# A four-layer transformer on one core: relative-position biases stored once, down rows paired, scores negated, scalings merged, block bias from Toeplitz tiles

## The chip, the core and the metric

The kernel runs on one core of one Trainium2 chip. Times are device microseconds (us) of one execution. Engines are called by their short names: PE is TensorE (PEld its weight loads), DVE VectorE, ACT ScalarE, POOL GpSimd, SP SyncE. A source line L196 is line 196 of the kernel before.

## The reference, cut to what matters

256 tokens of width 1,024 pass through four layers in float32. Layer 0 mixes by two kinds of attention (8 heads causal in one block, 8 heads dilated), layer 1 by a sparse attention of three branches (compressed, selected, windowed), and each of them is followed by a dense feed-forward net of 2,816 and a gated product. Layers 2 and 3 mix by attention in a band of 128 tokens with one sink per head beside a short convolution, followed by 32 experts of 512 of which each token uses two.

```python
s = einsum('bhqd,bhkd->bhqk', q, k) * HEAD_DIM ** -0.5 + tab[:, _rel_bucket(t_q - t_k)]
pr = exp(s - max(s)) / sum(exp(s - max(s)))          # masked to t_q >= t_k
o = einsum('bhqk,bhkd->bhqd', pr, v)
# layer 1, compressed branch: 15 keys, key c of tokens 16c .. 16c+31
dc = t[:, None] - (16 * arange(15) + 31)             # masked to dc >= 0
s = einsum('bghsd,bgcd->bghsc', qg, kc) * HEAD_DIM ** -0.5 + tabg[:, :, _rel_bucket(dc)]
# layers 2 and 3: sink in max and sum; experts: (silu(x @ gate) * (x @ up)) @ down
```

The bias depends on the distance of query and key alone, so a head's bias is one row of 256 numbers, and its 128 x 256 tile is that row shifted by one for each query: a Toeplitz tile.

## The kernel before, in words

The program is written out by hand: each engine runs its instructions in the order in which the Python code emits them, and waits on semaphores where a tile is not ready.

**Weights.** `Ring` loads them in pieces of 1 MB on SP's queue into a few slots (5 in the first two layers, with 8, 3 and 2 more from other pools later) in one fixed order; a piece is issued when a slot comes free. In the dense parts `Split` halves a piece into a high and a low part: ACT rounds it (`whi`, L196), DVE or, while `split.second` says so, POOL subtracts (`wlo`, L204), and PE multiplies three times (`mm3`, L332 to L334). The experts use the ring's pieces directly (L1728, L1752). Gate and up pieces have 8 KB in a row for each partition, down pieces two rows of 4 KB that lie 512 KB apart.

**Order.** `Side` holds generators that go a step further at each `tick`; a `yield 4` waits for four ticks. Layer 0 (`mixer0`) projects q, k, q, k and v in turn, PE working through pieces of the ring. Beside this `bias_rows` multiplies the table with a one-hot matrix, so that each head has its row (16 rows for the first kind, 8 with the dilation's weights), and POOL's queue writes each row 128 times to HBM (`rows_d`, 24 x 128 x 384). `bias_tiles` then reads a tile of four heads with a step of 383, which shifts each partition's row by one (`T`, two buffers, POOL's queue); the first two loads wait for the writes.

**Attention.** Units of two heads run through `Attention.run` at staggered offsets: scores on PE, `att_bias` on DVE (score plus bias, with the maximum of each row; L684, L686; then the maximum negated, L689), `att_exp` on ACT (L695, L696), `att_scale` on DVE (reciprocal, for layer 1 times the gate, then four scalings, L701 to L706), `att_transpose` on PE, `att_take` on ACT and DVE (`ta`, `tb`), values on PE. The output projection fills PE between the steps, with POOL subtracting its low parts. There are 8 units in layer 0 and 16 in layer 1.

**Behind layer 0's attention** `block_bias` loads two one-hot tiles on POOL's queue. In `last_steps` PE turns token tile 0, then makes 32 products of 32 rows by 16 columns (L979) for the bias of the compressed keys, which DVE adds to a mask (`cbias`), then turns token tile 1 (L369; ACT and DVE take the result, L381, L376, L385, L389), and `rest(0)` begins its feed-forward net (FFN 0), whose first product needs both tiles.

**Layers 2 and 3.** `mixer` does the banded attention inside a `Side` generator while the convolution's products fill PE; its scores are scaled by four instructions (L1385). `moe` takes the experts in pairs; `turn` transposes the activations of an expert in two halves of 128 columns (L1739), which meet the two down rows of a partition.

## Time and profile before

| | us |
|---|---|
| median of 3 runs | 1999.36 (1996.43 to 2000.14) |
| the profiled execution | 2000.12, its span 1998.4 |
| PE busy | 1816.1 (91%) |
| DVE busy | 835.6 (42%) |
| ACT busy | 679.5 (34%) |
| POOL busy | 135.8 (7%) |
| mean granted clock of PE | 0.968 |
| DMA | 559.15 MB, mean 280 GB/s over the span |

Matmuls are pipelined and their ends are modelled, so a busy PE is not PE at its peak. [...] The shares are means over stages with different limits.

### The profile page before, as it was taken

What the parts mean: (1) busy time and instruction counts of PE and PEld (TensorE: products, weight loads), DVE (VectorE), ACT (ScalarE), POOL (GpSimd) and SP (SyncE); (2) the same over time, 40 slices, a digit from 0 to 9 for tenths busy, and PEclk for the clock granted to TensorE, in tenths of its full rate; (3) what the DMA queues carried; (4) which work ended last, traced back from release to release, by engine and by line L of the source; (5) the groups of instructions that cost most, each with busy time, mean ns of one, the idle gap of its engine ahead of it and who ended that gap; (6) DMA issues with size and microseconds to landing.
All of it is one profiled execution on the core that took longest, in us unless ns stands there. A gap on an engine that the chain in (4) does not pass through costs nothing. (4 is left out here: it accounts for less than half of the span.)

```text
span 1998.4 us, 29447 instructions
## 1 busy us (share of the span) xinstructions
PE 1816.1 (91%) x11967; PEld 1399.4 (70%) x11967; DVE 835.6 (42%) x1918; ACT 679.5 (34%) x1415; POOL 135.8 (7%) x126
## 2 busy tenths in 40 slices
PE   8489999999889999997899999997897999998996
PEld 6367999877669998886677676563685777675553
DVE  6264655565866555695121121111684111121112
ACT  6154644564666445653111111111552111111111
POOL 0033000033320000200000000000110000000000
PEclk9788999999999999998999999999998999999999
DMA  9842655544226554574999999999845999999996
GB/s 248 164 151 83 232 190 191 168 131 146 71 64 232 190 193 166 175 273 166 379 417 417 416 416 417 416 417 402 315 169 203 388 416 416 417 416 417 417 416 272
DMA packets 170173, 559.15 MB, mean 280 GB/s; under 512 B 10176, under 2 KB 69992, under 8 KB 137200
## 3 DMA queue, kind: packets, MB, share of 16 engines
q1 hardware_dynamic: 167056, 546.47, 71.1%
q0 software_dynamic: 2976, 10.74, 3.2%
q8 instruction: 96, 1.57, 0.3%
q14 instruction: 45, 0.37, 0.1%
HBM read 551.40 MB, written 5.77 MB: 279 GB/s over the span
## 5 line engine op out<-in xcount | busy, mean ns | idle before, releaser
L1728 PE MATMUL wps<-wring,X 128*64 128x256 f32 x4096 | 480.6, 381 | 15.5 <-DMA wring<-in_w_expert_up_dram 15.3
L1728 PEld LDWEIGHTS wps<-wring,X 128*64 128x64 f32 x4096 | 336.3, 137 | 148.3 <-DMA wring<-in_w_expert_up_dram 30.4
L204 DVE TENSOR_TENSOR wlo<-wring,whi 128x1024 fp32r<-128x1024 f32 (+1 forms) x247 | 257.5, 1085 | 99.2 <-ACT whi L196 98.8
L196 ACT CAST whi<-wring 128x1024 fp32r<-128x1024 f32 (+1 forms) x283 | 254.8, 945 | 58.6 <-DMA wring<-in_w_in_ab_dram 39.7
L1752 PE MATMUL wps<-wring,aT 128*64 128x512 f32 x1024 | 250.6, 596 | 16.9 <-DMA wring<-in_w_expert_down_dram 16.9
L332 PE MATMUL wps<-xh,whi 128*128 128x256 f32 x832 | 236.0, 284 | 2.6 <-ACT xh L376 2.6
L333 PE MATMUL wps<-xl,whi 128*128 128x256 f32 x832 | 233.8, 281 | 1.4 <-DVE xl L389 1.4
L334 PE MATMUL wps<-xh,wlo 128*128 128x256 f32 x832 | 233.5, 281 | 0.0
L1733 DVE TENSOR_TENSOR a<-a,wps 128x256 f32<-128x256 f32 x64 | 27.0, 421 | 464.7 <-ACT a L1732 464.7
L1752 PEld LDWEIGHTS wps<-wring,aT 128*64 128x64 f32 x1024 | 116.9, 136 | 119.6 <-issue 49.9
L1732 ACT ACTIVATE a<-wps 128x256 f32<-128x256 f32 x64 | 24.6, 385 | 437.4 <-PE wps L1728 437.4
L332 PEld LDWEIGHTS wps<-xh,whi 128*128 128x128 f32 x832 | 157.6, 189 | 8.6 <-issue 3.3
L333 PEld LDWEIGHTS wps<-xl,whi 128*128 128x128 f32 x832 | 157.2, 189 | 3.3 <-DVE xl L389 1.9
L332 PE MATMUL acc<-whi,xh 128*128 128x512 f32 (+1 forms) x360 | 149.7, 416 | 8.9 <-ACT whi L196 8.9
L334 PEld LDWEIGHTS wps<-xh,wlo 128*128 128x128 f32 x832 | 157.8, 190 | 0.0
L1761 DVE SCALAR_TENSOR_TENSOR yl<-wps,gs,yh 128x512 fp32r<-128x512 f32 x64 | 48.0, 751 | 254.3 <-ACT yh L1760 252.7
L334 PE MATMUL acc<-whi,xl 128*128 128x512 f32 (+1 forms) x360 | 144.9, 402 | 8.2 <-DVE xl L389 7.9
L333 PE MATMUL acc<-wlo,xh 128*128 128x512 f32 (+1 forms) x360 | 144.7, 402 | 2.8 <-DVE wlo L204 2.8
L1760 ACT ACTIVATE yh<-wps,gs 128x512 fp32r<-128x512 f32 x64 | 43.9, 688 | 230.2 <-PE wps L1752 220.1
L347 POOL TENSOR_SCALAR ss<-ss 128x1 f32<-128x1 f32 x22 | 5.4, 244 | 1453.5 <-ACT junk L345 1453.3
L204 POOL TENSOR_TENSOR wlo<-wring,whi 128x1024 fp32r<-128x1024 f32 (+1 forms) x36 | 88.1, 2461 | 134.5 <-ACT whi L196 78.8
L334 PEld LDWEIGHTS acc<-whi,xl 128*128 128x128 f32 x360 | 71.0, 197 | 27.4 <-DVE xl L389 9.7
(367 smaller groups left out, 2492.8 us busy)
## 6 DMA issues: line engine op xcount, KB each, us to landing
wring<-in_w_expert_gate_dram SPq DMA_DIRECT2D x128, 1024.0 KB, 18.8
wring<-in_w_expert_up_dram SPq DMA_DIRECT2D x128, 1024.0 KB, 19.8
wring<-in_w_expert_down_dram SPq DMA_DIRECT2D x128, 1024.0 KB, 20.0
wring<-in_w_ffn_gate_dram SPq DMA_DIRECT2D x22, 1024.0 KB, 9.5
wring<-in_w_ffn_up_dram SPq DMA_DIRECT2D x22, 1024.0 KB, 5.4
wring<-in_w_ffn_down_dram SPq DMA_DIRECT2D x22, 1024.0 KB, 7.1
wring<-in_w_in_dram SPq DMA_DIRECT2D x18, 1024.0 KB, 8.6
wring<-in_w_in_ab_dram SPq DMA_DIRECT2D x10, 1024.0 KB, 11.5
```

The source lines that it names most:

```text
L196: self.nc.scalar.copy(vh, src)
L204: eng.tensor_sub(vl, src, vh)
L332: nc.tensor.matmul(o, lh, rh, start=start, stop=False)
L333: nc.tensor.matmul(o, lh, rl, start=False, stop=False)
L334: nc.tensor.matmul(o, ll, rh, start=False, stop=stop)
L347: nc.gpsimd.tensor_scalar(ss, ss, 1.0 / D, EPS, ALU.mult, ALU.add)
L1728: nc.tensor.matmul(o[64 * half:64 * half + 64, lo:lo + 256], xg[:, k, 64 * (e % 4):64 * (e % 4) + 64], w[:, c, 256 * half:256 * half + 256 ...
L1732: nc.scalar.activation(a, o[:, 0:256], AF.Silu)
L1733: nc.vector.tensor_mul(a, a, o[:, 256:512])
L1752: nc.tensor.matmul(y[d2][64 * ab:64 * ab + 64, :], aTs[ab][:, j, 64 * hf:64 * hf + 64], ws[ab][:, j, 512 * d2:512 * d2 + 512], start=hf + ...
L1760: nc.scalar.activation(ys[0][:, s_], y[d2], AF.Copy, scale=g)
L1761: nc.vector.scalar_tensor_tensor(ys[1][:, s_], y[d2], g, ys[0][:, s_], ALU.mult, ALU.subtract)
```

## The change

- `rows_d` holds each head's row once: 24 rows of 383 numbers, 127 masked ones ahead of the 256 biases, which now run in the order of the distance. A tile is read with a step of 1 from partition to partition (`toeplitz`), and `att_bias` reads it backwards along the keys.
- All scores are negated (the factor on q is -0.125, biases and masks change sign). The least value takes the place of the greatest and is already the offset that the exponent needs, which ACT evaluates with scale -1. The negations (L689, L1366) go. In the mixers a negated copy of the sinks is made on POOL.
- `att_scale` multiplies both heads at once by a broadcast operand, two instructions in place of four; the mixers' scaling becomes one in place of four.
- `block_bias` goes into `rest(0)` as a `Side` generator: two memsets, then four times a `toeplitz` load on POOL's queue, four ticks, and two DVE copies that pick every 16th column. The 32 products, the one-hot tiles and the mask go.
- Down pieces give each partition two neighbouring rows, 8 KB in one run; `turn` transposes the even and the odd columns.

```diff
...
-    c2["wmask"] = np.where(np.abs(t[:, :, None] - k) <= 128, 0.0, NEG).astype(f).reshape(128, -1)
+    c2["wmask"] = np.where(np.abs(t[:, :, None] - k) <= 128, 0.0, -NEG).astype(f).reshape(128, -1)
...
-    c["cmask"] = np.where(ok, 0.0, NEG).astype(f).reshape(128, -1)
...
-    hot = (np.arange(32)[:, None] == b[::-1]).astype(f)
-    bc = np.where(ok, b[np.maximum(dc, 0)], 0)
-    hotc = (np.arange(32)[:, None, None, None] == bc.transpose(1, 2, 0)).astype(f)
-    d = np.arange(S)[::-1]
+    hot = (np.arange(32)[:, None] == b).astype(f)
+    d = np.arange(S)
...
-    return c, c2, np.concatenate([hot, hotc.reshape(32, -1)], 1), np.broadcast_to(lnc, (8, S)).copy()
+    return c, c2, hot, np.broadcast_to(lnc, (8, S)).copy()
...
-                    ring.add(("d", l, e, hf), [(0, (2, 1024), x["w_expert_down_2"][l, e, 256 * hf:256 * hf + 256, :].rearrange("(c p) n -> p c n", p=128))])
+                    ring.add(("d", l, e, hf), [(0, (2, 1024), x["w_expert_down_2"][l, e, 256 * hf:256 * hf + 256, :].rearrange("(p c) n -> p c n", c=2))])
...
+            def keys(j, n):
+                v = T[:, 2 * hp + j, n - 1:n]
+                return bass.AP(tensor=v.tensor, offset=v.offset, ap=[v.ap[0], [-1, n]])
...
-                nc.vector.tensor_tensor_reduce(out=p[:, j, 0:256], in0=sc[j][:, 0:256], in1=T[:, 2 * hp + j, :], scale=1.0,
-                                               scalar=-3.0e38, op0=ALU.add, op1=ALU.max, accum_out=m[:, j:j + 1])
-                nc.vector.tensor_tensor_reduce(out=p[:, j, 256:384], in0=sc[j][:, 256:384], in1=T[:, 2 * hp + j, 128:256], scale=1.0,
-                                               scalar=-3.0e38, op0=ALU.add, op1=ALU.max, accum_out=m[:, 2 + j:3 + j])
-            nm = small.tile([128, 4], F32, name="nm", tag="nm")
-            nc.vector.tensor_scalar(nm, m, -1.0, None, ALU.mult)
-            return p, nm
+                nc.vector.tensor_tensor_reduce(out=p[:, j, 0:256], in0=sc[j][:, 0:256], in1=keys(j, 256), scale=1.0,
+                                               scalar=3.0e38, op0=ALU.add, op1=ALU.min, accum_out=m[:, j:j + 1])
+                nc.vector.tensor_tensor_reduce(out=p[:, j, 256:384], in0=sc[j][:, 256:384], in1=keys(j, 128), scale=1.0,
+                                               scalar=3.0e38, op0=ALU.add, op1=ALU.min, accum_out=m[:, 2 + j:3 + j])
+            return p, m
...
-                nc.scalar.activation(p[:, j, 0:256], p[:, j, 0:256], AF.Exp, bias=nm[:, j:j + 1], accum_out=l[:, j:j + 1])
-                nc.scalar.activation(p[:, j, 256:384], p[:, j, 256:384], AF.Exp, bias=nm[:, 2 + j:3 + j], accum_out=l[:, 2 + j:3 + j])
+                nc.scalar.activation(p[:, j, 0:256], p[:, j, 0:256], AF.Exp, scale=-1.0, bias=nm[:, j:j + 1], accum_out=l[:, j:j + 1])
+                nc.scalar.activation(p[:, j, 256:384], p[:, j, 256:384], AF.Exp, scale=-1.0, bias=nm[:, 2 + j:3 + j], accum_out=l[:, 2 + j:3 + j])
...
-            nc.vector.reciprocal(r, l)
...
+                nc.vector.reciprocal(r, l)
...
-            for j in range(2):
-                nc.vector.tensor_scalar(p[:, j, 0:256], p[:, j, 0:256], r[:, j:j + 1], None, ALU.mult)
-                nc.vector.tensor_scalar(p[:, j, 256:384], p[:, j, 256:384], r[:, 2 + j:3 + j], None, ALU.mult)
+            else:
+                nc.vector.reciprocal(r, l)
+            for i, s_ in enumerate((slice(0, 256), slice(256, 384))):
+                nc.vector.tensor_mul(p[:, :, s_], p[:, :, s_], r[:, 2 * i:2 * i + 2].unsqueeze(2).to_broadcast([128, 2, s_.stop - s_.start]))
...
+        def toeplitz(row, name, bufs):
+            t = ptile([128, 4, 256], F32, name, bufs=bufs)
+            nc.gpsimd.dma_start(t, bass.AP(tensor=rows_d.tensor, offset=rows_d.offset + row * 383, ap=[[1, 128], [383, 4], [1, 256]]))
+            return t
...
-                        tiles[i] = ptile([128, 4, 256], F32, "T")
-                        src = bass.AP(tensor=rows_d.tensor, offset=rows_d.offset + rows[i] * 128 * 384 + 127, ap=[[383, 128], [128 * 384, 4], [1, 256]])
-                        nc.gpsimd.dma_start(tiles[i], src)
+                        tiles[i] = toeplitz(rows[i], "T", 2)
...
-        def last_steps(i, outp, nxt, pp, pv, mid=None):
+        def last_steps(i, outp, nxt, pp, pv):
...
-            if mid:
-                fns.append(mid)
-            for k in sorted(range(len(fns)), key=lambda k: (15 if k == 5 else T1[11 + 6 * i + k])):
+            for k in sorted(range(len(fns)), key=lambda k: T1[11 + 6 * i + k]):
...
-        rows_d = dram.tile([24, 128, 384], F32, name="rows_d")
+        rows_d = dram.tile([24, 383], F32, name="rows_d")
...
-            nc.sync.dma_start(hot, x["hot"][:, 0:256])
+            nc.sync.dma_start(hot, x["hot"])
...
-            nc.gpsimd.memset(r1[:, 256:], NEG)
-            nc.gpsimd.memset(r2[:, 256:], NEG)
+            nc.gpsimd.memset(r1[:, :127], -NEG)
+            nc.gpsimd.memset(r2[:, :127], -NEG)
...
-            nc.vector.tensor_copy(r1[:, :256], pr[:16, 0:256])
-            nc.vector.tensor_add(r2[:, :256], pr[:8, 256:512], lnc)
-            nc.gpsimd.dma_start(rows_d[0:16], r1.unsqueeze(1).to_broadcast([16, 128, 384]))
-            nc.gpsimd.dma_start(rows_d[16:24], r2.unsqueeze(1).to_broadcast([8, 128, 384]))
+            nc.vector.tensor_scalar(r1[:, 127:383], pr[:16, 0:256], -1.0, None, ALU.mult)
+            nc.vector.scalar_tensor_tensor(r2[:, 127:383], pr[:8, 256:512], -1.0, lnc, ALU.mult, ALU.subtract)
+            nc.gpsimd.dma_start(rows_d[0:16], r1[:, :383])
+            nc.gpsimd.dma_start(rows_d[16:24], r2[:, :383])
...
-            hotc = [ptile([128, 16, 128], F32, "hotc", tag=tag, bufs=1) for tag in ("qT", "kT")]
-            for i in range(2):
-                nc.gpsimd.dma_start(hotc[i][:32].rearrange("p a b -> p (a b)"), x["hot"][:, 256 + 2048 * i:2304 + 2048 * i])
-            yield 0
-            pc = wps()
-            for i in range(32):
-                nc.tensor.matmul(pc[:, 16 * i:16 * i + 16], hotc[i // 16][:32, i % 16, :], M["tab"][:32, :], start=True, stop=True)
-            for t in range(2):
-                nc.vector.tensor_add(cbias[:, t], pc[:, 256 * t:256 * t + 256].rearrange("p (c h) -> p h c", c=16),
-                                     C["cmask"][:, 16 * t:16 * t + 16].unsqueeze(1).to_broadcast([128, 16, 16]))
-            yield 0
+            nc.gpsimd.memset(cbias[:, 0, :, 7:], -NEG)
+            nc.gpsimd.memset(cbias[:, 1, :, 15:], -NEG)
+            for q in range(4):
+                T = toeplitz(4 * q, "Tb", 1)
+                yield 4
+                for t, n in ((0, 7), (1, 15)):
+                    v = T[:, :, 16 * n - 16:16 * n - 15]
+                    nc.vector.tensor_copy(cbias[:, t, 4 * q:4 * q + 4, 0:n], bass.AP(tensor=v.tensor, offset=v.offset, ap=[v.ap[0], v.ap[1], [-16, n]]))
...
-                nc.vector.tensor_scalar(gq[:, i:i + 1], M[a], M[b], 0.125, ALU.mult, ALU.mult)
+                nc.vector.tensor_scalar(gq[:, i:i + 1], M[a], M[b], -0.125, ALU.mult, ALU.mult)
...
-            bb = block_bias()
-            next(bb)
...
-            last_steps(0, outp, nm, pp, pv, lambda: next(bb))
+            last_steps(0, outp, nm, pp, pv)
...
+                if i == 0:
+                    side.spawn(block_bias())
...
-            nc.vector.tensor_scalar(gq, M["qn_nsa"], 0.125, None, ALU.mult)
+            nc.vector.tensor_scalar(gq, M["qn_nsa"], -0.125, None, ALU.mult)
...
-                nc.vector.tensor_reduce(out=mx, in_=pc, axis=AX.X, op=ALU.max)
+                nc.vector.tensor_reduce(out=mx, in_=pc, axis=AX.X, op=ALU.min)
...
-                nc.scalar.activation(pc, pc, AF.Exp)
+                nc.scalar.activation(pc, pc, AF.Exp, scale=-1.0)
...
+            nsink = ptile([128, 8], F32, "nsink", bufs=1)
+            nc.gpsimd.tensor_scalar(nsink, sink, -1.0, None, ALU.mult)
...
-                                                       scalar=sink[:, 2 * hp + j:2 * hp + j + 1], op0=ALU.add, op1=ALU.max, accum_out=m[:, j, t:t + 1])
-                nc.vector.tensor_scalar(m, m, -1.0, None, ALU.mult)
+                                                       scalar=nsink[:, 2 * hp + j:2 * hp + j + 1], op0=ALU.add, op1=ALU.min, accum_out=m[:, j, t:t + 1])
...
-                        nc.scalar.activation(p[:, j, t], p[:, j, t], AF.Exp, bias=m[:, j, t:t + 1], accum_out=l_[:, j, t:t + 1])
+                        nc.scalar.activation(p[:, j, t], p[:, j, t], AF.Exp, scale=-1.0, bias=m[:, j, t:t + 1], accum_out=l_[:, j, t:t + 1])
...
-                for j in range(2):
-                    for t in range(2):
-                        nc.vector.tensor_scalar(p[:, j, t], p[:, j, t], l_[:, j, t:t + 1], None, ALU.mult)
+                nc.vector.tensor_mul(p, p, l_.unsqueeze(3).to_broadcast([128, 2, 2, 256]))
...
-                nc.scalar.activation(qT[:, :, 128 * t:128 * t + 128], pt.rearrange("p (c n) -> p c n", c=4), AF.Copy, scale=0.125)
+                nc.scalar.activation(qT[:, :, 128 * t:128 * t + 128], pt.rearrange("p (c n) -> p c n", c=4), AF.Copy, scale=-0.125)
...
-                    nc.tensor.transpose(pt[:, 128 * j:128 * j + 128], a[:, 128 * j:128 * j + 128], ident)
+                    nc.tensor.transpose(pt[:, 128 * j:128 * j + 128], a.rearrange("p (m j) -> p j m", j=2)[:, j], ident)
...
```

## Rows read from the trace of the kernel before

**Rows 1.** the page's slices: what the DMA engines moved, GB/s in 40 slices of 50 us

```profile
GB/s 248 164 151 83 232 190 191 168 131 146 71 64 232 190 193 166 175 273 166 379 417 417 416 416 417 416 417 402 315 169 203 388 416 416 417 416 417 417 416 272
```

**Rows 2.** windows: length, busy us and instructions by engine, TensorE's granted clock, DMA share, GB/s

```profile
20.00:60.00 40.00, 40.00 (x185) 31.59 (x184) 26.34 (x49) 19.28 (x29) 2.32 (x2) 1.00 1.01 181
60.00:110.00 50.00, 19.81 (x73) 14.88 (x73) 13.30 (x19) 12.52 (x18) 1.56 (x2) 0.66 0.76 199
```

**Rows 3.** DMA issues by line: engine, count, KB of each, median us from issue to landing

```profile
T<-rows_d POOLq DMA_DIRECT2D x8, 512.0 KB, 5.2
rows_d<-r POOLq DMA_DIRECT2D x1, 3072.0 KB, 37.5
rows_d<-r POOLq DMA_DIRECT2D x1, 1536.0 KB, 68.6
```

**Rows 4.** waits from 60 to 101 us: who waited for whom, total us, times, longest

```profile
ACT whi L196 <- DMA wring<-in_w_in_ab_dram: 39.0, 3, 23.3
```

**Rows 5.** timeline behind the first attention: start, us, engine, line, operation [idle <-releaser]

```profile
187.99 10.59 PE L979 MATMUL wps<-sm,hotc 32*128 32x16 f32 x64
189.34 0.92 ACT L376 CAST xh<-xn 128x256 fp32r<-128x256 f32 x2
198.51 1.97 PE L369 MATMUL wps<-idg,xn 128*128 128x128 f32 x8
199.66 0.63 ACT L381 ACTIVATE xn<-wps,sm 128x128 f32<-128x128 f32 x2 [9.40 <-PE wps L369]
200.77 0.58 PE L332 MATMUL wps<-xh,whi 128*128 128x256 f32 x1 [0.30 <-ACT xh L376]
```

**Rows 6.** windows over the two attentions, as rows 2

```profile
110.00:178.00 68.00, 58.51 (x310) 41.41 (x311) 36.63 (x131) 34.61 (x96) 32.57 (x22) 0.92 0.37 118
490.00:600.00 110.00, 93.30 (x608) 69.30 (x604) 84.60 (x313) 64.64 (x201) 34.80 (x29) 0.97 0.21 66
```

**Rows 7.** windows at the start of FFN 0, as rows 2

```profile
202.00:204.00 2.00, 1.98 (x9) 1.98 (x10) 1.73 (x3) 2.00 (x3) 0.00 (x0) 0.50 0.00 0
206.00:208.00 2.00, 2.00 (x19) 2.00 (x18) 2.00 (x3) 2.00 (x4) 0.00 (x0) 1.00 0.66 96
```

**Rows 8.** VectorE's groups, second attention: xcount | busy us, mean ns | idle before

```profile
L705 DVE TENSOR_SCALAR p<-p,r 128x256 f32<-128x256 f32 x32 | 13.6, 426 | 0.6
L689 DVE TENSOR_SCALAR nm<-m 128x4 f32<-128x4 f32 x16 | 12.5, 781 | 0.6
L706 DVE TENSOR_SCALAR p<-p,r 128x128 f32<-128x128 f32 x32 | 9.0, 280 | 0.0
L703 DVE TENSOR_TENSOR r<-r,gates 128x4 f32<-128x4 f32 x16 | 5.5, 344 | 0.5
```

**Rows 9.** VectorE's groups, first attention (110 to 178 us)

```profile
L689 DVE TENSOR_SCALAR nm<-m 128x4 f32<-128x4 f32 x8 | 7.7, 966 | 0.3
```

**Rows 10.** the negation alone: ns min/median/max, first and last start

```profile
L689 DVE TENSOR_SCALAR nm<-m x24: 170/171/2359, 112.1 to 573.7; 128x4 f32<-128x4 f32 x24
```

**Rows 11.** GpSimd's groups, 480 to 605 us

```profile
L204 POOL TENSOR_TENSOR wlo<-wring,whi 128x1024 fp32r<-128x1024 f32 x14 | 33.7, 2411 | 21.3 <-ACT whi L196 21.3
```

**Rows 12.** VectorE's two-input products by shape, 480 to 605 us

```profile
L389 DVE TENSOR_TENSOR xl<-xn,xh 128x256 fp32r<-128x256 f32 x4 | 1.6, 419 | 0.2 <-ACT xh L376 0.2
L389 DVE TENSOR_TENSOR xl<-xn,xh 128x512 fp32r<-128x512 f32 x2 | 1.4, 693 | 0.1
```

**Rows 13.** waits of TensorE's weight loads, second attention

```profile
PEld wps L725 <- DVE tb L719: 6.6, 6, 2.6
```

**Rows 14.** the mixers' scalings: ns min/median/max, first and last start

```profile
L1385 DVE TENSOR_SCALAR X<-X,l x32: 340/348/753, 850.1 to 1476.4; 128x256 f32<-128x256 f32 x32
```

**Rows 15.** DMA queues, 1848.3 to 1858.5 (down) and 1860 to 1878 us: packets, MB, share

```profile
q1 hardware_dynamic: 973, 4.21, 102.6%
...
q1 hardware_dynamic: 1123, 7.50, 100.6%
```

**Rows 16.** expert weight issues from 1590 to 1960 us: ns, first and last start

```profile
L143 SPq DMA_DIRECT2D wring<-in_w_expert_down_dram x51: 367/379/2440, 1592.5 to 1957.9; - x51
```

## The prediction, made before the changed kernel was run

> **What bounds the kernel now.** I read the slices of the page first, for the stages. HBM traffic stands near 417 GB/s from 1,000 to 1,400 us and again from 1,600 to the end: the two expert stages run at the speed of the DMA engines [rows 1]. Before 1,000 us the traffic is lower and TensorE sets the pace, with one exception at the start: between 60 and 110 us the traffic sags and TensorE does little. The windows show it: 73 matmuls in those 50 us at a granted clock of 0.66, against 185 in the 40 us before at 1.00 [rows 2]. The issues say why: the two writes of `rows_d`, 3.0 and 1.5 MB out of 16 and 8 partitions, take 37.5 and 68.6 us to land [rows 3], and meanwhile the first projection's weights are late: ScalarE, which rounds them, waits 39.0 us for them in three waits [rows 4]. The reader should see that nothing else is due in that stretch. Third, the timeline behind the first attention: the 32 small products of `block_bias` stand between the turns of token tile 0 and of tile 1, and FFN 0 begins only after both [rows 5]. Fourth, the two attention stages: TensorE is busy 58.5 of 68 and 93.3 of 110 us, VectorE 84.6 of the 110 [rows 6].
>
> **The change part by part.** The sum is made against the profiled execution's 2000.1 us, 0.8 above the median of 1999.4.
>
> *Biases once.* The writes shrink from 4.5 MB to 24 rows of 1.5 KB, 37 KB in all; at any rate the trace shows that is hidden under the projections. Then 60 to 110 us goes at the pace of 20 to 60 us: 73 matmuls at 40/185 us each are 15.8 us instead of 50.0, a gain of 34.2. What hides the weights afterwards is the same ring that kept TensorE 100% busy from 20 to 60 us [rows 2]. Bounds: if the clock stays where it was, the busy 19.8 us remain and 30.2 are gained; if transposes, which are shorter, count less, 36.
>
> *Block bias moved.* [...] Without it the transposes of tile 1 go at 188.0 instead of 198.5. ScalarE is busy with tile 0 until 190.26 and then needs the 1.1 us from 199.66 to 200.77 again, so FFN 0 starts at 191.4 instead of 200.77: 9.4. FFN 0 then began at half clock (9 matmuls in 2 us at 202, 19 at 206 [rows 7]); some 3 us of it at twice the speed are 1.5 more. I take 10.8; 8.3 if the wait after the transposes stays 2.26 us behind ScalarE's last cast, 12 at best. The step moves into FFN 0: two memsets, four loads of 512 KB on GpSimd's queue and eight copies of at most 60 elements on VectorE. GpSimd has no other work there, the loads have four steps of FFN 0 to land where a tile of this size needs 5.2 us [rows 3], and behind the waiting load stands nothing but the next one. I cost it at nothing; were the cover gone, eight copies at some 0.2 us are 1.6 us.
>
> *Negation dropped, scalings merged.* `L689`, four numbers per partition, should take 0.17 us and takes 0.966 and 0.781 on average in the two attentions, with a maximum of 2.359 [rows 8 to 10]: as long as one GpSimd subtraction, 2.41 us [rows 11]. So it queues behind GpSimd. All 24 are 20.2 us of VectorE. The scalings of the second attention, 32 x 0.426 and 32 x 0.280, are 22.6 us; merged, 16 products of 512 at 0.693 and 16 of 256 at 0.419 [rows 12] are 17.8. Eight units of the first attention save about 2.4 in proportion. VectorE loses 27.4 us in all; TensorE's idle time there, 9.5 + 16.7 us [rows 6], is what can be won from that. The largest wait of its weight loads in the second attention names VectorE (6.6 us for `tb` [rows 13]), but only 24 x 0.17 of the negations was work; the rest was waiting for GpSimd, which the merged product may have to do instead: a product of four numbers, `L703`, takes 0.344 on average in the same stretch [rows 8]. I take a third of the idle time, 9; bounds nothing and 20.
>
> [...]
>
> *The hybrid mixers.* Four scalings at 0.348 [rows 14] and one negation at 0.17 become one product of 1,024, about 1.24 (0.419 and 0.693 continued): 0.3 saved for each of 8 head pairs, 2.6 us of VectorE. Convolution matmuls stand between the attention's steps there, so I take 0.8 of it; between nothing and 2. The negated sinks are one tiny GpSimd instruction each.
>
> *Down rows paired.* Each partition's two rows of 4 KB become one run of 8 KB, the form that gate and up already have. Two windows filled by one kind each give the price: 102.6% of 10.2 us for 4.21 MB of down, 100.6% of 18.0 us for 7.50 MB of gate and up [rows 15]. Per load of 1.049 MB that is 2.607 against 2.532 us, 0.075 saved. I take 0.065, since the windows' edges cut packets. It counts where the DMA queue is the bound: behind TensorE's first expert pair, 51 of layer 1's 64 down loads are issued in one unbroken stream [rows 16]; with as many in layer 0 that is 102 x 0.065 = 6.6 us. Bounds: nothing if bytes alone set the rate, 128 x 0.075 = 9.6. The transposes that go with it read every second column. Eight transposes take 1.97 us at half clock [rows 5], 0.12 each at full; if all 128 took twice as long, that is 16 us of TensorE over two stages of some 400 us that the DMA engines limit [rows 1]. I cost them at nothing.
>
> [...]
>
> Sum: 34.2 + 10.8 + 9 + 0.8 + 6.6 = 61.4 off 2000.1, less the 0.8 to the median: 1938.
>
> **Rivals.** (a) *The wait for GpSimd only moves.* The merged products queue behind GpSimd's 2.41 us as the negation did, and attention gains nothing: 1947. For it: the `L703` row; against it: the 24 negations and half of the 96 scalings are gone and can't queue. [...]
> (b) *VectorE was the bound of both attentions*, and 20 us come back: 1927. For it: 84.6 of 110 us; against: part of TensorE's idle time names ScalarE.
> (c) *Runs of 8 KB bring nothing*: 1945. For it: both stretches move about 417 GB/s [rows 1]; against: the packets' own time [rows 15].
> (d) *The start finds another bound*, ring slots or ScalarE, and 10 us of the 34 stay: 1948. Against it: 40 us at 100%.
> (e) *The reversed reading of `T` halves VectorE's rate there.* Then 24 units pay 2 x (0.274 + 0.137) = 0.82 us, by the step from 256 to 512 elements [rows 12], 19.7 in all, attention's gain is gone, and the time is 1967. Nothing in the trace reads backwards, so it can't be excluded.
> (f) *Slower than before: the bias tiles come from one 37 KB table.* All 512 runs of a tile now read the same few KB of HBM. If a tile then lands in X us, the two later tiles of each attention, loaded only when a buffer comes free, two units of 68/8 us ahead, are each X - 17 late. From X = 32 the 61.4 us are gone, and at the 69 us of the slowest landing in the trace [rows 3] the time would be 1938 + 4 x 52 = 2146. Against it: 5.2 us today for the same 512 runs.
>
> **How the numbers follow.** Chances: forecast 0.38, (a) 0.22, (b) 0.13, (c) 0.13, (d) 0.07, (e) 0.05, (f) 0.02. All but (e) and (f) lie between 1927 and 1948. All good bounds together (36 + 12 + 20 + 2 + 9.6) give 1920, all bad ones (30.2 + 8.3) 1961; half-way combinations of them set the range, 1922 to 1956. A change of 0.2%, 4 us, is about what a measurement of this kernel tells from none. Only (f), or a failed first term together with (e), could bring that: faster 0.97, same 0.01, slower 0.02.
>
> **What would show it.** TensorE busy without a gap to the first scores, which come near 76 us instead of 110; `rows_d` landing within a few us. No product of 32 rows behind the first attention, and 1.00 in PEclk there. `L689`'s successor gone and the merged products at 0.69 and 0.42 us: means far above would be (a). Down loads at 8 KB, with the same GB/s over a shorter stretch. I would be wrong first in the attention term, which rests on a guess of one third, and most dearly if `T` is read or landed slower than today.

## The result and the profile after

The changed kernel takes 1929.64 us (median of 4 runs, 1928.09 to 1931.81) against 1999.75 us beside it: ratio 0.9653, 95% interval [0.9637, 0.967]. 70 us are gone where 61.4 were forecast.

Where they went is read best from the start times of a few lines in both traces, as steps between marks (us, after minus before; the two profiled spans are 70.8 apart): up to the first score products -35.6; from there to the last head of the first attention -10.6; to the first activation of FFN 0 -9.6; the second attention -3.3; the two expert stages -3.7 and -3.6; the rest -4.4 in small steps of both signs. Such a step carries some 2 us of chance: e6 and e7 below, whose edits lie in the experts, reach the last head of the first attention 2.0 and 1.5 us later than this profile. The windows of the changed kernel, as in [rows 2] and [rows 6]:

```profile
20.00:60.00 40.00, 40.00 (x188) 32.10 (x187) 29.80 (x52) 23.08 (x34) 2.83 (x4) 1.00 0.73 248
60.00:76.00 16.00, 16.00 (x79) 12.90 (x78) 10.49 (x21) 9.68 (x15) 0.00 (x0) 1.00 0.49 178
...
74.00:142.00 68.00, 63.06 (x362) 46.54 (x361) 40.42 (x123) 40.65 (x114) 33.56 (x26) 1.00 0.37 120
432.00:540.00 108.00, 94.15 (x612) 71.88 (x611) 79.40 (x268) 65.36 (x203) 35.44 (x29) 0.95 0.21 70
```

TensorE now works without a gap at a granted clock of 1.00 (full speed) up to the first scores, which start at 74.3 us. In the first attention it is busy 63.06 of 68 us where it was 58.51, and the clock has gone from 0.92 to 1.00. VectorE is no less busy there than before (40.42 against 36.63): more of the work falls into the same 68 us.

The DMA issues of the start (after [rows 3]; columns as there) show the new table and its tiles landing in under 5 us at the median (4.0 to 7.0 for all eight tiles of the attentions):

```profile
T<-rows_d POOLq DMA_DIRECT2D x4, 512.0 KB, 4.7
...
rows_d<-r POOLq DMA_DIRECT2D x1, 23.9 KB, 4.9
rows_d<-r POOLq DMA_DIRECT2D x1, 12.0 KB, 4.4
```

VectorE's groups by shape: two of the kernel before in the first attention (110 to 178 us), then of the changed kernel the first attention (74 to 142 us) and the second (432 to 540 us). Behind the bar stand busy us, the mean of one in ns, and the idle time before:

```profile
L684 DVE CUSTOM_DVE_ANT_0 p<-wps,T 128x256 f32<-128x256 f32 x16 | 6.7, 419 | 1.5 <-PE wps L677 1.5
L686 DVE CUSTOM_DVE_ANT_0 p<-wps,T 128x128 f32<-128x128 f32 x16 | 4.6, 285 | 0.0
```

```profile
L709 DVE TENSOR_TENSOR p<-p,r 128x512 f32<-128x512 f32 x8 | 12.4, 1549 | 0.3
L688 DVE CUSTOM_DVE_ANT_0 p<-wps,T 128x256 f32<-128x256 f32 x16 | 6.7, 421 | 2.3 <-PE wps L674 2.3
L690 DVE CUSTOM_DVE_ANT_0 p<-wps,T 128x128 f32<-128x128 f32 x16 | 4.6, 285 | 0.0
...
L709 DVE TENSOR_TENSOR p<-p,r 128x512 f32<-128x512 f32 x16 | 11.1, 692 | 0.6
L709 DVE TENSOR_TENSOR p<-p,r 128x256 f32<-128x256 f32 x16 | 11.0, 690 | 0.0
L705 DVE TENSOR_TENSOR r<-r,gates 128x4 f32<-128x4 f32 x16 | 8.3, 522 | 0.5
```

Two things stand here. The biases with the reversed tile (L688, L690) take 421 and 285 ns where they took 419 and 285: reading backwards costs nothing. And the wait that the negation had [rows 9] has moved: the 512-wide merged product takes 1549 ns in the first attention, where 692 ns is its time in the second; there the 256-wide one takes 690 ns, where 414 ns is its time in the first. The attention gained all the same. One thing that has changed is seen in the timeline of one unit (start, duration in us, engine, line):

```profile
79.06 0.42 DVE L688 CUSTOM_DVE_ANT_0 p<-wps,T 128x256 f32<-128x256 f32 x1 [0.22 <-PE wps L674]
...
79.53 0.51 ACT L697 ACTIVATE p<-p,m 128x256 f32<-128x256 f32 x1 [1.03 <-DVE m L688]
...
80.17 0.08 DVE L690 DVE_READ_ACCUMULATOR2_ANT m<- 128x1 f32 x1
```

ScalarE starts the first exponent at 79.53 when the first of the four least values is there; the fourth is read at 80.17. With a negation of all four in between, no exponent could start before the fourth: in the trace of e1 a unit's fourth value is read at 81.35, and its first exponent starts at 82.65. What this overlap is worth is tested in e12.

### The profile page after: what moved, and what is told of

Read it like the earlier page. It is cut to its first block, busy times and chain, and to the rows that moved or that the text cites. A ratio compares the mean times of both kernels' runs of the same rounds, so it can differ in the third digit from the quotient of the medians.

```text
span 1927.6 us, 29217 instructions
## 1 busy us (share of the span) xinstructions
PE 1788.6 (93%) x11903; PEld 1393.7 (72%) x11903; DVE 824.8 (43%) x1820; ACT 679.5 (35%) x1415; POOL 137.2 (7%) x132
## 5 line engine op out<-in xcount | busy, mean ns | idle before, releaser
L1728 PE MATMUL wps<-wring,X 128*64 128x256 f32 x4096 | 480.7, 381 | 13.6 <-DMA wring<-in_w_expert_up_dram 13.6
L1728 PEld LDWEIGHTS wps<-wring,X 128*64 128x64 f32 x4096 | 340.4, 137 | 140.9 <-DMA wring<-in_w_expert_up_dram 26.5
L193 ACT CAST whi<-wring 128x1024 fp32r<-128x1024 f32 (+1 forms) x283 | 254.9, 945 | 23.5 <-PE acc L331 11.7
```

What stands on the lines that cost most here:

```text
L193: self.nc.scalar.copy(vh, src)
L1728: nc.tensor.matmul(o[64 * half:64 * half + 64, lo:lo + 256], xg[:, k, 64 * (e % 4):64 * (e % 4) + 64], w[:, c, 256 * half:256 * half + 256 ...
```

## The experiments

Each run's ratio is to the kernel before, timed beside it; the last column is the difference of that ratio from 0.9653, times 1999 us. Each interval is some 3 us to either side, so a difference to the changed kernel carries about 4 us. e1 to e4, e5 to e8 and e9 to e11 were each timed on one chip, e12 on another, and the medians are compared only within these groups.

| run | what differs from the changed kernel | median us | ratio, interval | us |
|---|---|---|---|---|
| e1_neg | extra tensor_scalar on the least values | 1943.04 | 0.9721 [0.9708, 0.9735] | +14 |
| e2_neg_reduce | the same by a reduction | 1934.60 | 0.9674 [0.9661, 0.9687] | +4 |
| e3_unmerged | scalings not merged | 1928.22 | 0.9649 [0.9636, 0.9663] | -1 |
| e4_unattn | e1 and unmerged attention | 1942.27 | 0.9714 [0.9701, 0.9727] | +12 |
| e5_writes | old broadcast writes, unread | 1960.27 | 0.9807 [0.9792, 0.9822] | +31 |
| e6_unpaired | down rows unpaired | 1937.25 | 0.9696 [0.9683, 0.9709] | +9 |
| e7_gu4k | gate and up in 4 KB runs | 1943.18 | 0.9721 [0.9708, 0.9734] | +14 |
| e8_blockold | 32 products back in place | 1939.20 | 0.9705 [0.9692, 0.9718] | +10 |
| e9_lowvec | low parts on VectorE | 1930.22 | 0.9653 [0.9639, 0.9666] | 0 |
| e10_neg_lowvec | e1 and e9 | 1941.89 | 0.9714 [0.97, 0.9727] | +12 |
| e11_ttrscale | scalings by the fused instruction | 1930.01 | 0.9657 [0.9644, 0.967] | +1 |
| e12_lastfirst | exponents in another order | 1931.47 | 0.9656 [0.9643, 0.9669] | +1 |

### The attention edits, one by one (e1 to e4)

```diff
-            return p, m
+            nm = small.tile([128, 4], F32, name="nm", tag="nm")
+            nc.vector.tensor_scalar(nm, m, 1.0, None, ALU.mult)
+            return p, nm
```

> The changed kernel with one more VectorE instruction in each of the 24 units of the two attentions: a 128x4 tensor_scalar that multiplies the least values by 1.0 before ScalarE takes them (the place and the form of the negation that the change dropped); nothing else differs. Theory, the wait behind GpSimd: the instruction must wait for GpSimd's low parts as the negation did (966 ns mean in the first attention, some 170 where GpSimd is idle), so its mean is 0.6 us or more in the first attention, and because ScalarE's exponents stand behind it, the kernel loses 5 to 9 us, most of it in the two attentions. Rival, only one more short instruction on the chain: 24 x 0.17 us = 4 us at most, and since TensorE is busy for most of the stretch, 0 to 3 us.

```diff
...
+            nc.vector.tensor_reduce(out=nm, in_=m.unsqueeze(2), axis=AX.X, op=ALU.min)
```

> As the run with the extra tensor_scalar, but the same 128x4 values are passed on by a VectorE reduction over an axis of one element, a kind of instruction of which the traces so far show none that waits behind GpSimd. Theory, the wait behind GpSimd: it takes some 0.1 to 0.25 us each, and the kernel loses 0 to 3 us, less than half of what the extra tensor_scalar costs. Rival, any further instruction on the chain from the least values to the exponents costs alike: the same loss as the extra tensor_scalar within 1.5 us.

The extra instruction alone, first attention: durations min/median/max, first of the run with the tensor_scalar, then of the one with the reduction, and VectorE's group in the former:

```profile
L693 DVE TENSOR_SCALAR nm<-m x8: 169/650/2311, 77.0 to 120.4; 128x4 f32<-128x4 f32 x8
```

```profile
L693 DVE TENSOR_REDUCE nm<-m x8: 157/157/159, 76.6 to 117.4; 128x4 f32<-128x4 f32 x8
```

```profile
L693 DVE TENSOR_SCALAR nm<-m 128x4 f32<-128x4 f32 x8 | 7.6, 947 | 0.3
L711 DVE TENSOR_TENSOR p<-p,r 128x512 f32<-128x512 f32 x8 | 6.9, 858 | 0.3
```

Both stand in the same place and do the same. One varies between 169 and 2311 ns, as [rows 10] did, the other never leaves 157 to 159, and they are 8.4 us apart (1940.57 to 1945.49 against 1928.09 to 1935.86). The wait is the difference that their traces show, and by it some 8 us of e1's loss are the wait's, though no run of this kernel has the tensor_scalar without its wait (e10 has it where VectorE does other work besides). The loss of e1 sits where expected: its trace loses 8.9 us in the first attention and 4.7 in the second. That e1 costs more than the 5 to 9 us of the theory may come from the place itself, which the reduction pays too; its +4 is no more than its uncertainty, and its five times lie apart, two at 1928 to 1930 and three at 1935 to 1936. While the negation waits, the products behind it wait less: 858 ns instead of 1549.

```diff
-            for i, s_ in enumerate((slice(0, 256), slice(256, 384))):
-                nc.vector.tensor_mul(p[:, :, s_], p[:, :, s_], r[:, 2 * i:2 * i + 2].unsqueeze(2).to_broadcast([128, 2, s_.stop - s_.start]))
+            for j in range(2):
+                nc.vector.tensor_scalar(p[:, j, 0:256], p[:, j, 0:256], r[:, j:j + 1], None, ALU.mult)
+                nc.vector.tensor_scalar(p[:, j, 256:384], p[:, j, 256:384], r[:, 2 + j:3 + j], None, ALU.mult)
```

(and the same in the mixers)

> The changed kernel with the four scalings of each attention unit back in place of the two merged products, and the four of each head pair back in the hybrid mixers. Theory, that the merging carries about half of the attentions' gain and the dropped negation the other half: 3 to 7 us slower, all but 1 us of it in the two attentions. Rival, that the merging brings nothing since the wait for GpSimd has only moved to the merged products (1549 ns in the first attention, where 692 ns is their time in the second): within 2 us of the changed kernel, or faster in the first attention.

> The changed kernel with both attention edits taken back at once: the extra 128x4 tensor_scalar on the least values, and the four scalings in place of the two products (the hybrid mixers stay merged). Theory: the two attentions lose together what they gained in the trace, 11 to 15 us, and the loss is more than that of the two single edits added up, because each alone leaves VectorE room for the other. Rival, the two edits are independent: the loss is the sum of the two single runs within 2 us. Second rival, that much of the attentions' gain came from the clock and the earlier start and not from these edits: 8 us or less.

Merging brings nothing that can be measured, in the attentions or the mixers: -1 us when it is undone, and no mark moves by 3 us. The theory that it carried half of the gain fell. Both undone give +12, the sum of +14 and -1 within the uncertainty: the two edits are independent, as the first rival of e4 had it. In the trace of e4 the first attention loses 10.4 us and the second 2.6, about what they had gained, and the granted clock of the first is back at 0.92. So the gain and the clock belong to these edits and not to the earlier start; the second rival is out.

### Who makes the negation wait, and what that is worth (e9 to e12)

```diff
             values(0, proj2("ab", 2, 4))
-            split.second = nc.gpsimd
...
             side.spawn(heads(o, 8, False, qT[:, 0:4], gq))
-            split.second = nc.gpsimd
```

> The changed kernel with the low parts of the weights made by VectorE instead of GpSimd in the two attentions (and in the projections just ahead of the second one), 1226 ns each on VectorE where GpSimd takes 2421 ns; nothing else differs. Theory, that what VectorE's products, copies and scalings wait for is GpSimd at work: the merged 128x512 product falls from 1549 to some 690 ns in the first attention and the gate's 128x4 product from 522 to some 170 ns in the second. For the time both theories leave little: VectorE takes on 10 x 1.23 us in each attention and gives back some 7 us of waits, so -3 to +6 us. Rival, that those means are long for a reason of their own (their operands in the accumulator, their broadcast operand): they stay where they are.

With GpSimd's subtractions gone (POOL busy 9.45 instead of 33.56 of the 68 us), the merged product of the first attention is back at its own time:

```profile
L709 DVE TENSOR_TENSOR p<-p,r 128x512 f32<-128x512 f32 x8 | 5.5, 692 | 0.3
```

The gate's product and the 256-wide one of the second attention come down too, from 522 and 690 ns:

```profile
L709 DVE TENSOR_TENSOR p<-p,r 128x256 f32<-128x256 f32 x16 | 6.7, 419 | 0.0
L705 DVE TENSOR_TENSOR r<-r,gates 128x4 f32<-128x4 f32 x16 | 2.6, 163 | 0.5
```

So the long means were waits for GpSimd at work; the rival fell. The time did not move, 0 us: in the changed kernel these waits cost nothing, or no more than VectorE's added low parts took back.

> The run with the low parts on VectorE, and the extra 128x4 tensor_scalar on the least values in it as well. Theory, that the dropped negation gained by the wait behind GpSimd alone: with GpSimd idle the extra instruction takes some 0.17 us and costs 0 to 4 us beside the run with the low parts on VectorE, where beside the changed kernel it cost 13.4 us (8.9 us in the first attention). Rival, that a place in VectorE's queue between the least values and the exponents costs that much whatever GpSimd does: 10 us or more beside the run with the low parts on VectorE.

```profile
L693 DVE TENSOR_SCALAR nm<-m x8: 170/170/172, 76.7 to 120.6; 128x4 f32<-128x4 f32 x8
```

The instruction no longer waits, 170 to 172 ns each, and still the run is 11.7 us over e9 (1938.09 to 1941.95 against 1926.9 to 1931.83). The theory that the negation was dear by that wait alone fell, and its rival's number came out. In these two kernels VectorE makes the low parts itself (12 of 1.22 us in the first attention), so that whatever is late on the chain from scores to exponents may meet a fuller queue; that is argued, not shown, and the reduction was not tried here. The traces of e9 and e10, which lie 6.8 us apart, place 4.9 us of it in the first attention, where TensorE's waits for the least values grow from 0.5 to 2.0 us; the other 5 us of the 11.7 are not in the profiled executions, and no run places them.

```diff
-                nc.vector.tensor_mul(p[:, :, s_], p[:, :, s_], r[:, 2 * i:2 * i + 2].unsqueeze(2).to_broadcast([128, 2, s_.stop - s_.start]))
+                nc.vector.tensor_tensor_reduce(out=p[:, :, s_], in0=p[:, :, s_], in1=r[:, 2 * i:2 * i + 2].unsqueeze(2).to_broadcast([128, 2, s_.stop - s_.start]),
+                                               scale=1.0, scalar=-3.0e38, op0=ALU.mult, op1=ALU.max, accum_out=l[:, i:i + 1])
```

> The changed kernel with the two merged products of a unit and the gate's product made by the fused instruction that the biases use (product, and a greatest value that nobody reads, which goes to sums that have been used up). Its traces show no such instruction waiting behind GpSimd (421 and 285 ns beside a busy GpSimd). Theory, that the waits which the dropped negation handed on to the scalings lie where nothing stands behind them: the scalings' 128x512 falls from 1549 to about 0.8 us in the first attention, the gate's product from 522 to about 0.25 us in the second, and the time stays within 2 us. Rival, that these waits still set the pace: 3 to 8 us faster, in the two attentions.

```profile
L709 DVE CUSTOM_DVE_ANT_1 p<-p,r 128x512 f32<-128x512 f32 x8 | 12.4, 1548 | 0.3
L688 DVE CUSTOM_DVE_ANT_0 p<-wps,T 128x256 f32<-128x256 f32 x16 | 6.7, 421 | 3.0 <-PE wps L674 3.0
...
L705 DVE CUSTOM_DVE_ANT_0 r<-r,gates 128x4 f32<-128x4 f32 x16 | 8.4, 523 | 0.5
```

The expectation was wrong about the instruction: the fused form waits exactly as long as the plain one, 1548 and 523 ns. One thing that differs from the biases, which never wait (L688 takes 410 to 426 ns in all 48 of the changed kernel), is where the operands lie: L688 reads one from the accumulator (`wps`), L709 both from SBUF. That this is the cause was not shown. The run says nothing on the theory about the time, since the waits stayed; of the runs only e9 bears on it.

```diff
-            for j in range(2):
-                nc.scalar.activation(p[:, j, 0:256], p[:, j, 0:256], AF.Exp, scale=-1.0, bias=nm[:, j:j + 1], accum_out=l[:, j:j + 1])
-                nc.scalar.activation(p[:, j, 256:384], p[:, j, 256:384], AF.Exp, scale=-1.0, bias=nm[:, 2 + j:3 + j], accum_out=l[:, 2 + j:3 + j])
+            for j, i in ((1, 1), (0, 0), (0, 1), (1, 0)):
+                s_ = slice(256, 384) if i else slice(0, 256)
+                nc.scalar.activation(p[:, j, s_], p[:, j, s_], AF.Exp, scale=-1.0, bias=nm[:, 2 * i + j:2 * i + j + 1], accum_out=l[:, 2 * i + j:2 * i + j + 1])
```

> The changed kernel with the four exponents of each attention unit in another order: the one that belongs to the last of the four least values first, then the other three as they were; no instruction is added. In the trace of the changed kernel a unit's first exponent starts up to 0.73 us before its four biases are through, since it needs only the first least value; in the kernel before, and in every run with an instruction between the least values and the exponents, it started some 0.25 us after them. With this order it can start only when all four are there, as in those runs, but nothing waits for GpSimd and VectorE does nothing more. Theory, that part of what the dropped negation gained is this overlap of biases and exponents: 3 to 6 us slower (the run with the reduction lost 5 us), 2 to 4 us of it in the first attention. Rival, that the overlap is worth nothing and the loss was the extra instruction's own time and its wait for GpSimd: within 1.5 us of the changed kernel.

+1 us: less than the theory's 3, and too near to nothing for a verdict against the rival. Its trace does lose 3.6 us in the first attention, with TensorE busy 10.11 of the 15 us from 90 to 105 at a clock of 0.77, and gives 2.2 us back elsewhere; the profile of the changed kernel has 1.00 there:

```profile
90.00:105.00 15.00, 10.11 (x46) 7.26 (x45) 10.73 (x29) 7.71 (x24) 6.92 (x6) 0.77 0.44 146
```

```profile
90.00:105.00 15.00, 10.94 (x72) 7.88 (x71) 10.71 (x39) 10.18 (x32) 6.82 (x6) 1.00 0.33 113
```

By the ratio and its uncertainty the lost overlap alone is worth at most some 4 us.

ScalarE's waits ahead of a unit's first exponent in the first attention can be compared over the runs: 7.5 us in the changed kernel and 6.7 in e9, 10.4 in e12, 11.1 in e10, 11.4 in e2, 15.8 in e1. The 3 to 4 us more than in the changed kernel or, for e10, in e9 go with +1 us in e12, +4 in e2 and +12 in e10. So this wait alone does not set the price of the extra instruction.

### The start, the experts' runs and the block bias (e5 to e8)

```diff
...
+            nc.gpsimd.dma_start(rows_b[0:16], r1.unsqueeze(1).to_broadcast([16, 128, 384]))
+            nc.gpsimd.dma_start(rows_b[16:24], r2.unsqueeze(1).to_broadcast([8, 128, 384]))
...
```

> The changed kernel with the old traffic put back and nothing that waits for it: the 24 rows are also written 128 times each into a second region of DRAM that nobody reads (4.7 MB, the two broadcast writes of the kernel before), while the bias tiles are still read from the compact copy. Theory, that the start was late because of that traffic: the weights of the first projection arrive later, the first score products start at about 110 us instead of 74 us, and the kernel loses 30 to 37 us. Rival, that the start was late because the bias tiles had to wait for the rows to land: 0 to 5 us.

Its issues at the start, and its largest wait from 60 to 101 us:

```profile
rows_b<-r POOLq DMA_DIRECT2D x1, 3072.0 KB, 36.4
rows_b<-r POOLq DMA_DIRECT2D x1, 1536.0 KB, 68.3
T<-rows_d POOLq DMA_DIRECT2D x2, 512.0 KB, 68.4
```

```profile
ACT whi L193 <- DMA wring<-in_w_in_ab_dram: 39.4, 3, 23.1
```

The writes land as slowly as before, ScalarE waits 39.4 us for the weights where it waited 39.0 [rows 4], and 31 us are lost. The tiles land late as well here, behind the writes on the same queue, but nobody's wait names them: it is the traffic. The first scores start at 104.3 us, 5.6 earlier than before; that rest of the start was not traced further.

```diff
-                    ring.add(("d", l, e, hf), [(0, (2, 1024), x["w_expert_down_2"][l, e, 256 * hf:256 * hf + 256, :].rearrange("(p c) n -> p c n", c=2))])
+                    ring.add(("d", l, e, hf), [(0, (2, 1024), x["w_expert_down_2"][l, e, 256 * hf:256 * hf + 256, :].rearrange("(c p) n -> p c n", p=128))])
...
-                    nc.tensor.transpose(pt[:, 128 * j:128 * j + 128], a.rearrange("p (m j) -> p j m", j=2)[:, j], ident)
+                    nc.tensor.transpose(pt[:, 128 * j:128 * j + 128], a[:, 128 * j:128 * j + 128], ident)
```

> The changed kernel with the down projections of the experts loaded again as rows p and p + 128, 4 KB runs, and the transposes in front of them reading neighbouring elements. Theory, a fixed price of each packet: a 1 MB load of 4 KB runs takes about 0.07 us longer than one of 8 KB runs, and 102 of the loads count, so 6 to 8 us slower, all of it in the two expert stages. Rival, that the queue moves bytes at one rate whatever the runs: within 1 us, or faster by the shorter weight loads of the transposes (0.056 us x 128 = 7 us at the very most if none were hidden).

```diff
-                        ring.add((nm, l, e, hf), [(0, (4, 512), w[l, e].rearrange("(p k) f -> p k f", k=8)[:, 4 * hf:4 * hf + 4, :])])
+                        ring.add((nm, l, e, hf), [(0, (2, 1024), w[l, e].rearrange("(q p k) f -> p q (k f)", q=4, k=2)[:, 2 * hf:2 * hf + 2, :])])
```

> The changed kernel with the gate and up weights of the experts loaded in 4 KB runs instead of 8 KB runs (each partition takes two pairs of neighbouring rows in place of four rows; the tokens are not rearranged to match, so these products meet other rows of the weights and the outcome is not the reference's; instructions and bytes are the same). Theory, a fixed price of each packet: 256 such loads of 1 MB, of which some 205 to 250 are in the stretches where the queue sets the pace, at 0.07 us each: 14 to 18 us slower, and the expert stages' rate falls by some 2.5%. Rival, that the runs of the down loads counted for another reason than their packets: 0 to 3 us.

SP's queue from 1550 to 1850 us, packets, MB and share of the 16 engines: the changed kernel, then e6, then e7:

```profile
q1 hardware_dynamic: 17267, 125.75, 100.9%
```

```profile
q1 hardware_dynamic: 22096, 124.64, 101.4%
```

```profile
q1 hardware_dynamic: 27165, 123.41, 101.8%
```

All three keep the 16 engines full for the 300 us, at 420, 416 and 412 GB/s. 4,829 packets more move 1.11 MB (0.88%) less, 9,898 more 2.34 MB (1.86%) less: 0.0088 and 0.0186 of 4,800 engine-microseconds, 9 ns for each packet by either run. A 1 MB load has 8 packets more per engine in 4 KB runs, by an estimate from these counts 0.07 us. In the trace of e6 each expert stage loses 4.1 us, in that of e7 6.8 and 8.1. Bytes alone do not set the rate; both rivals fell. The weight loads of the transposes (L1740) take 196 ns at the median with the strided reading, and took 140 without it in the kernel before (L1739); the 7 us at most that this could cost do not show, since e6 lost time in both stages.

```diff
...
+                for i in range(32):
+                    nc.tensor.matmul(pc[:, 16 * i:16 * i + 16], hotc[:32, i % 2, :], M["tab"][:32, :], start=True, stop=True)
...
```

(between the two halves of the last transposes, as [rows 5], with two copies behind it)

> The changed kernel with 32 products of 32 rows put back between the two halves of the last transposes in front of the first dense layer, where the kernel before had its block bias, with their 16 KB load and the two copies out of the accumulator; the block bias itself is still the Toeplitz one, which overwrites their values. Theory: TensorE spends some 10 us there at a lower granted clock, as the kernel before did (10.59 us on one product's line), and the kernel loses 8 to 12 us, all of it ahead of the first dense layer's first activation. Rival, that the products cost their own short time and the former stretch was a wait for the load of 512 KB that came with them: 1 to 4 us.

Its timeline behind the first attention, then windows there:

```profile
149.67 4.21 PE L1045 MATMUL wps<-sm,hotc 32*128 32x16 f32 x19
...
154.96 0.62 ACT L378 ACTIVATE xn<-wps,sm 128x128 f32<-128x128 f32 x2 [9.94 <-PE wps L366]
```

```profile
150.00:160.00 10.00, 9.03 (x40) 8.30 (x40) 4.67 (x11) 4.98 (x10) 1.18 (x3) 0.50 0.15 54
160.00:162.00 2.00, 2.00 (x12) 2.00 (x11) 2.00 (x3) 2.00 (x3) 0.00 (x0) 0.50 0.02 2
162.00:164.00 2.00, 2.00 (x15) 2.00 (x15) 2.00 (x3) 2.00 (x3) 0.00 (x0) 0.79 0.89 272
```

ScalarE again waits 9.9 us for the second tile's transposes (9.40 in [rows 5]), the clock stands at 0.50 from 150 to 160 us, and FFN 0 runs its first microseconds at 0.50 and 0.79 too. With 32 KB loaded (32 rows of 256 numbers, not the 16 KB of the expectation) in place of 512 KB the price is the same, +10 us: the theory held, the wait for a load is out. The lower clock at the start of FFN 0 is not the products' alone, though: the changed kernel, without them, has it too, if for a shorter time (1.00 again from 150 to 152 us). TensorE is idle there for most of 142 to 146 us (busy 1.02 of the 4, the clock at 1.00), waiting for the second tile, and then runs as these windows show:

```profile
146.00:148.00 2.00, 1.90 (x10) 1.90 (x11) 1.70 (x4) 2.00 (x3) 0.00 (x0) 0.59 0.00 0
148.00:150.00 2.00, 2.00 (x12) 2.00 (x12) 2.00 (x3) 2.00 (x3) 0.00 (x0) 0.56 0.00 0
```

## Why the prediction was right, point by point

**Biases once**, 34.2: the trace gained 35.6 and the traffic alone is worth 31 (e5). TensorE goes at 40 us per 188 matmuls right through to 76 us; rival (d), another bound at the start, did not come. The mechanism held.

**Block bias moved**, 10.8: 9.6 in the trace, +10 when the products are put back (e8). All of it lies ahead of FFN 0's first product. The 1.5 us that the term hoped for from FFN 0 at full clock, and the sign of a clock of 1.00 there, did not come: 0.59 and 0.56 from 146 to 150 us. The step into FFN 0 cost nothing: the four tiles landed in 4.2 to 7.6 us, the eight copies took 177 to 217 ns.

**Down rows paired**, 6.6: 7.3 in the two stages, +9 with an uncertainty of 4 when undone (e6); rival (c) is out, and no stage shows a cost of the transposes. A packet costs 9 ns on the full queue by the traces of e6 and e7.

**Negation dropped, scalings merged**, 9: this is the mis-sized term, 13.9 in the trace and +12 when undone (e4). The step took VectorE's 27.4 us of lost work as the source and a third of TensorE's idle time as the share, and said itself that the third was a guess; that 9 came near is luck. VectorE's load was not the source: 7.2 us of the 27.4 (22.6 less 17.8, and 2.4) were to come from merging, and merging is worth nothing that can be measured (e3). Nor did it save that time on VectorE. The merged products of the second attention take 11.1 + 11.0 = 22.1 us, not 17.8, because the 256-wide one waits; in e9, where VectorE makes the low parts and GpSimd is busy for 9.60 of the 108 us instead of 35.44, they do take 17.8, and that run gained nothing either. In the first attention they take 15.7 us, where the scalings took 6.9 + 6.7 = 13.6.

The prediction also took 0.426 us for the work of a scaling of 256, against 0.693 for a product of 512. The scalings of the kernel before (min/median/max, both attentions) show waits in that mean:

```profile
L705 DVE TENSOR_SCALAR p<-p,r x48: 339/352/2498, 114.4 to 578.9; 128x256 f32<-128x256 f32 x48
L706 DVE TENSOR_SCALAR p<-p,r x48: 267/280/2485, 114.6 to 579.1; 128x128 f32<-128x128 f32 x48
```

At 352 ns two scalings take as long as one product of 512, 0.70 against 0.69 us. From 128 to 256 elements a scaling grows by 72 ns, from 256 to 512 a product by 274 [rows 12], so by an estimate from these times an element costs a scaling 0.56 ns and a product 1.07, and some 0.2 of the scaling's 0.35 us do not depend on its elements.

The gain, within the uncertainty, came from the one short instruction between the least values and the exponents (e1, e4). The bound on it was also drawn too narrowly: the term counted TensorE's idle time alone, and left out the clock. In the first attention the idle time fell from 9.5 to 4.9 us of 68, and the granted clock rose from 0.92 to 1.00; by an estimate from these rows the clock is worth 58.5 x 0.08 = 4.7 us, as much as the idle time. Rival (a) described what happened, the products wait for GpSimd instead, 1549 ns, but its conclusion that the attention gains nothing was wrong. Taking the waits at the scalings away gained nothing (e9), while the same wait ahead of the exponents goes with about 8 us (e1 against e2). Rival (b), 1927, lies near the measured time for a wrong reason.

**The hybrid mixers**, 0.8: the merging there brings nothing measurable (e3 undid it too). Their dropped negation was undone in no run; the trace gains 1.6 and 1.4 us in the two mixers and gives 0.5 and 1.1 back before the first expert's activation. Rivals (e) and (f) are out by rows of the trace after: L688 at 421 ns, and tiles in 4.0 to 7.0 us.

The four terms undone singly (31 + 10 + 12 + 9 = 62) do not quite add up to the 70; 5.6 of the difference is the start that e5 did not give back. Open is also how the price of the place itself arises: a bare reordering costs 1 us, a reduction 4, a tensor_scalar without a wait 12 where VectorE has the low parts to do. That the short instruction carried the gain is shown; by what chain it did so is shown only in part.

## What to carry to other kernels

Price an instruction by undoing it, not by its share of its engine: 24 instructions with 0.17 us of work each (20.2 us with their waits) were worth 12 to 14 us, while 22.6 us of scalings could be rearranged without effect. Look at the median beside the mean before you count a saving: what is waiting in the mean moves elsewhere. When a wait moves, look where to; here its new place cost nothing that could be measured. And look at what a small thing does to its surroundings: two writes that 16 and 8 partitions feed held up the weights for 39 us, and 32 products of 32 rows took 10.59 us of TensorE [rows 5] at a clock that fell to 0.50 (196 to 200 us, kernel before).

## What the runs showed of the hardware that was not expected

- In the traces of the kernel before and of the changed one, the VectorE instructions that read the accumulator stay within 13 ns of their median line by line, and those that reach 1 us or more beside a median far below it (up to 2143 ns at L705, 6225 at L709 in the changed kernel) read SBUF alone; with GpSimd's subtractions gone these two come down to means of 163 and, at 512 elements, 692 ns (e9). In e11: 1548 ns for the fused instruction on two SBUF operands, 421 ns for the same family with one operand in the accumulator. Reading SBUF alone is not enough, though: a reduction of 128x4 there never waited (157 to 159 ns, e2), a tensor_scalar of the same shape did, up to 2311 ns (e1).
- A further packet cost 9 ns on the full queue (100.9 to 101.8% of the 16 engines), the same whether one third (e6) or two thirds (e7) of an expert's weights went from 8 to 4 KB runs.
- A second input read backwards cost VectorE nothing: 421 and 285 ns for the biases, 419 and 285 before. The copies that read every 16th element took 177 to 217 ns for 28 and 60 elements; no run has them without the step.
